# Chunks of the activations without padding, each pair of parts at a place of its own modulo 512 bytes

## The chip, the cores and the metric

The kernel runs on one core of one Trainium2 chip. The metric is the device time of one execution in microseconds. Before the change the median of three runs is 751.33 us (750.96 to 751.88).

## What is computed

The input x has 256 tokens of 1,024 channels. Two different transformer blocks run one after the other, in float32, and a root-mean-square norm stands between them.

The first block: norm, one input projection, then two mixers side by side (block attention with 8 heads of 64 and rotary positions; gated linear attention with 4 heads, a per-token decay and an output gate), a projection w_out back to 1,024 channels and a residual sum. Then norm, an up projection to 2 x 2,816 channels, a causal convolution over 3 tokens, silu(gate) x value, a down projection to 1,024 and a residual sum.

The second block: norm, one input projection that feeds four mixers (short convolution, spatial gating, stick-breaking attention, forgetting attention, each 256 wide) and four gates of 1,024; each mixer's result is projected to 1,024, multiplied with its sigmoid gate and summed; a projection w_out_2 and a residual sum; then a SwiGLU of the same width as the first FFN and a residual sum.

```
h = causal_dwconv(hn @ w_ffn_up, conv_w, conv_b)
x = x + (silu(h_gate) * h_val) @ w_ffn_down
...
merged = sum(gates * branches, axis=2);  h = h + merged @ w_out
h = h + (silu(g) * u) @ w_out_ffn,  g, u = split(norm(h) @ w_ffn_in)
```

## The kernel before

Activations lie with channels on the 128 partitions and tokens along the free axis: 1,024 channels are KD = 8 chunks of 256 tokens, 2,816 channels KF = 22 chunks. A chunk is 256 float32, so 1,024 bytes per partition.

Precision is kept by splitting each operand into a high and a low part: the high part is the value rounded to TensorE's faster float32 form (F32R), the low part the rest. A product is three matmuls (`mm3`, lines 184 to 187): high x high, low x high and high x low. In most stages the weight tile of 128x128 is the stationary operand and a chunk of 128x256 the moving one (`fm`, `fm_pair`); in the four value projections (`tm`) it is the other way round.

The weights, 117 pieces of 1 MB, stream through `raws` (3 buffers) on SP's DMA queue. `Stream.split_to` (lines 145 to 160) makes from each half piece a high part with ScalarE (line 154) and a low part with VectorE (line 155), in `parts`, 5 buffers of 128x1024 each; a half holds 8 weight tiles of 512 bytes per partition. `Stream.tiles` (line 162) hands the tiles out in the order in which the layout on the host has put them, so the order of the matmuls is the order of the program.

The activations' parts live in four tiles of the pool `bigs`, made by `new_x` (xh, xl) and `new_y` (yh, yl), lines 297 to 301. Each such tile has 8 chunks with 8 float32 of padding behind each, so chunk k begins 1,056 k bytes into the tile. They are made anew several times, in the order of the program: xh, xl for the first projections, for the held columns of FFN one, for the mixers' results of the second block (the branches) and for the rest of FFN two; yh, yl for the mixers' results of the first block (w_out), for the rest of FFN one, for the projections of the second block and for the held columns of FFN two. `Boundary` (lines 377 to 424) makes the parts behind each residual sum: first unnormed ones, with which the first HELD = 6 column pairs of the FFN are computed and scaled afterwards, then the normed ones for the other 16. The hidden values of an FFN stand in hh, hl (line 762), 22 chunks with 4 float32 of padding behind each, 1,040 bytes apart. The input of w_out_2, mh and ml (lines 1075 and 1076), has no padding.

Results land in PSUM; VectorE, ScalarE and GpSimd scale, convolve, gate and split them while the next matmuls run. The work of the mixers is written as generators that `pump` advances by a step after every four chunks. lv (line 81) holds the masks that the gated linear attention's six levels read (line 548); its load is one of four in `late_loads` (line 91) on SP's queue.

Of the kernel before, what the change touches and what calls it, by code (L numbers as in the profile page):

```python
# [10 lines left out]
F32R = mybir.dt.float32r  # L11
BF = mybir.dt.bfloat16
I32 = mybir.dt.int32
# [5 lines left out]
D, T, FF = 1024, 256, 2816  # L19
KD, KF = D // 128, FF // 128  # L20
# [7 lines left out]
LEVELS = (1, 2, 4, 8, 16, 32)  # L28
# [24 lines left out]
def block_kernel(ctx: ExitStack, tc: tile.TileContext, xT, wst, sm_d, cs_d, lv_d, gup_d, out, dbg=None):  # L53
    nc = tc.nc
# [3 lines left out]
    def pool(name, bufs, **kw):  # L58
        return tc.tile_pool(name=name, bufs=bufs, reuse_waits="tile", **kw)

    const = ctx.enter_context(tc.tile_pool(name="const", bufs=1))
# [6 lines left out]
    def mm_tile():  # L68
        return mmp.tile([128, 512], F32, name="mm", tag="mm")

    def at_tile():
        return atp.tile([128, 512], F32, name="at", tag="at")
# [5 lines left out]
    X = resid.tile([128, KD, T], F32, name="X")  # L78
    sm = const.tile([128, SM_W], F32, name="sm")
    cs = const.tile([128, CS_W], F32, name="cs")  # L80
    lv = const.tile([128, len(LEVELS), 64], I32, name="lv")
    gup = const.tile([17, 256], F32, name="gup")
    nc.scalar.dma_start(out=sm[:, :SM_FIRST], in_=sm_d[:, :SM_FIRST])

# [6 lines left out]
    def late_loads():  # L91
        nc.sync.dma_start(out=cs, in_=cs_d)
        nc.sync.dma_start(out=sm[:, SM_FIRST:], in_=sm_d[:, SM_FIRST:])
        nc.sync.dma_start(out=lv, in_=lv_d)
        nc.sync.dma_start(out=gup, in_=gup_d)

    def par(name):
# [74 lines left out]
    st = Stream()  # L172
    st.load_to(3)
    late_loads()
    identb = const.tile([128, 128], BF, name="identb")
    V.tensor_copy(identb, ident)
# [12 lines left out]
    def fm(ps, xh, xl, ks, start=True, stop=True, steps=0, **kw):  # L189
        ks = list(ks)  # L190
        for n, k in enumerate(ks):
            wh, wl = st.tiles()
            mm3(ps, wh, wl, xh[:, k, :], xl[:, k, :], start and n == 0, stop and n == len(ks) - 1, **kw)
            if n % 4 == 3:
                pump(steps)

    def fm_pair(ps, xh, xl, between=None):

        for n, (a, k) in enumerate([(a, k) for a in range(2) for k in range(KD - 1)] + [(0, KD - 1), (1, KD - 1)]):
            wh, wl = st.tiles()  # L200
            mm3(ps[:, a * T:(a + 1) * T], wh, wl, xh[:, k, :], xl[:, k, :], n == 0, k == KD - 1,
                skip_group_check=True)
            if between and n == KD:
                between()
# [11 lines left out]
    def split_from(h, l, src):  # L216
        S.copy(h, src)
        V.tensor_tensor(l, src, f32(h), op=ALU.subtract)
# [75 lines left out]

    bigs = ctx.enter_context(tc.tile_pool(name="bigs", bufs=1))

    def new_x():
        return tuple(bigs.tile([128, KD, T + 8], F32R, name=n, tag=n)[:, :, :T] for n in ("xh", "xl"))

    def new_y():  # L300
        return tuple(bigs.tile([128, KD, T + 8], F32R, name=n, tag=n)[:, :, :T] for n in ("yh", "yl"))

    nwk = ctx.enter_context(tc.tile_pool(name="nwk", bufs=1))

# [72 lines left out]
    class Boundary:  # L377


        def __init__(self, g, sums=None, first=None, then=None):  # L380
            self.g, self.then = g, then or new_x
            self.h, self.l = (first or new_y)()
            self.ss = SumSq(nwk, "a")
            self.s2, self.g2 = (SumSq(nwk, "b"), sums) if sums is not None else (None, None)
# [18 lines left out]
        def finish(self):  # L403
            if self.s2 is None:
                v, t = (nwk.tile([128, T], F32, name="sq", tag="sq", bufs=3) for _ in range(2))
                self.rb = nwk.tile([128, T], F32, name="rb", tag="rb", bufs=2)
                V.tensor_scalar(v, self.p1, 1.0 / D, EPS, op0=ALU.mult, op1=ALU.add)
                newton(v, self.rb, t, True)
                return
            else:  # L410
                tc.keep_in_program_order(S.preload_act_table_set("natural_log_exp_and_others"))

                v = nwk.tile([128, 4], F32, name="v4")
                V.tensor_scalar(v[:, 0:2], self.p1, 1.0 / D, EPS, op0=ALU.mult, op1=ALU.add)
                V.tensor_scalar(v[:, 2:4], v[:, 0:2], EPS, None, op0=ALU.mult)
                V.scalar_tensor_tensor(v[:, 2:4], self.p2, 1.0 / D, v[:, 2:4], op0=ALU.mult, op1=ALU.add)
                r = inv_sqrt(v, 4, nwk)
                self.r1, r = r[:, 0:2], r[:, 2:4]
            self.r = r
            self.rb = spread(r, nwk)  # L420
# [6 lines left out]


    with pool("first", 1) as wk:
        ss = SumSq(nwk, "a")  # L430
        xh, xl = new_x()
        for k in range(KD):
            scaled(k, par("g_attn"), xh, xl)
# [16 lines left out]
        V.scalar_tensor_tensor(gq, pss[0].rearrange("p (a t) -> p a t", a=2), 0.125, rbb, op0=ALU.mult, op1=ALU.mult)  # L450
        V.tensor_tensor(gk, pss[1].rearrange("p (a t) -> p a t", a=2), rbb, op=ALU.mult)
        yh, yl = new_y()
        cosr = wk.tile([128, T], F32, name="cosr")
        sinr = wk.tile([128, T], F32, name="sinr")
# [281 lines left out]
        if "ya" in dbg:  # L736
            drain(t_gla)
            for k in range(KD):
                t = wk.tile([128, T], F32, name="dbgt")
# [5 lines left out]
        for half in range(2):  # L745
            for d in range(KD):
                a = accs[d // 2]
                fm(a[:, (d % 2) * T:(d % 2 + 1) * T], yh, yl, range(4 * half, 4 * half + 4),
                   start=(half == 0 and d % 2 == 0), stop=(half == 1), steps=2, skip_group_check=True)
                if half and d % 2:  # L750
                    if d == 1:
                        nb_ = Boundary(par("g_ffn"), first=new_x, then=new_y)
                    for e in (d - 1, d):
                        nb_.add(e, a[:, (e % 2) * T:(e % 2 + 1) * T])
            drain(t_gla)
# [3 lines left out]
    def gated_ffn(nb, emit, finish):  # L759

        with pool("ffn", 1) as wk:
            hh, hl = (wk.tile([128, KF, T + 4], F32R, name=n)[:, :, :T] for n in ("hh", "hl"))
            held = []

            def hidden(ps, j):
                split_from(hh[:, j, :], hl[:, j, :], emit(ps, j, wk))

            for j in range(KF):
                ps = mm_tile()
                if j == 0:  # L770
                    fm_pair(ps, nb.h, nb.l, nb.sums)
                    nb.finish()
                    nb.normed()
                else:
                    x = (nb.h, nb.l) if j < HELD else (nb.xh, nb.xl)
                    for half in range(2):
                        fm(ps[:, half * T:(half + 1) * T], *x, range(KD))
                if j < HELD:
                    t = wk.tile([128, 2, T], F32, name="held", tag="held", bufs=3)
                    V.tensor_tensor(t, ps.rearrange("p (a t) -> p a t", a=2),  # L780
                                    nb.rb[:, None, :].to_broadcast([128, 2, T]), op=ALU.mult)
                    hidden(t.rearrange("p a t -> p (a t)"), j)
                else:
                    hidden(ps, j)
            for d in range(KD):
                ps = mm_tile()
                fm(ps[:, :T], hh, hl, range(KF))
                finish(d, ps[:, :T], wk)
# [24 lines left out]
    def first_end(d, ps, wk):  # L813
        if not holder:
            holder.append(Boundary(ggm, par("g_fin")))
        holder[0].add(d, ps)

    gated_ffn(nb_, conv_emit, first_end)
    nb_ = holder[0]

    with pool("second", 1) as wk:
        yh, yl = new_x()
        fr = [wk.tile([128, 2, T], F32, name="fr", tag="t2", bufs=4) for _ in range(2)]
        pss = []
# [11 lines left out]
        xh, xl, rb, r = nb_.h, nb_.l, nb_.rb, nb_.r  # L839
# [22 lines left out]
        pl = at_tile()  # L862
# [31 lines left out]
        for hd in range(2):  # L894
            p, m = 64 - 64 * hd, 96 - 64 * hd
# [214 lines left out]
        if "yb" in dbg:  # L1110
            for k in range(KD):
                t = wk.tile([128, T], F32, name="dbgt")
# [28 lines left out]
    def second_end(d, ps, wk):  # L1141
        V.tensor_tensor(X[:, d, :], X[:, d, :], ps, op=ALU.add)
        nc.sync.dma_start(out=out[:, d, :], in_=X[:, d, :])

    gated_ffn(nb_, swiglu_emit, second_end)
    assert st.used == 16 * N_PIECES, st.used

# [158 lines left out]
```

## Time and profile before

| | |
|---|---|
| median of three runs | 751.33 us |
| profiled execution | 751.71 us |
| its span | 750.0 us |
| TensorE matmul busy | 736.9 us, 6,042 instructions |
| VectorE busy | 535.8 us |
| ScalarE busy | 423.2 us |
| GpSimd busy | 113.9 us |
| DMA | 127.51 MB, 170 GB/s |
| granted TensorE clock | 0.995 of full speed |

PE is TensorE, PEld its weight loads, DVE VectorE, ACT ScalarE, POOL GpSimd, SP the engine that issues the DMAs. Busy time adds the durations of an engine's instructions, overlaps counted once. A matmul's duration covers its whole way through the array and overlaps the next one's, so the distance between two starts is shorter than a duration. An L with a number is a line of the kernel.

### The profile page before, as it was taken

The page shows a single profiled execution, that of the slowest core. Times are in us where ns is not written, and L with a number is a line of the kernel's source. Part 1 is how long each engine was busy: PE and PEld are TensorE (multiplying, and loading weights), DVE is VectorE, ACT ScalarE, POOL GpSimd, SP SyncE. Part 2 cuts the span into 40 slices and gives each one's busy share as a digit, 9 for nine tenths or more (in the row PEclk, how much of TensorE's full clock was granted, in tenths as well). Part 3 has the DMA queues.
Part 4 walks back from the last instruction along what each step waited for, and adds up shares of the span by engine and source line. Part 5 has one row for each costly group of instructions (what it writes and reads, how often), then busy time and mean ns, then how long its engine had stood idle before and what let it go on. Part 6 is the DMA issues. An engine that isn't in the chain of part 4 may idle for free.

```text
span 750.0 us, 14591 instructions
## 1 busy us (share of the span) xinstructions
PE 736.9 (98%) x6042; PEld 718.9 (96%) x6042; DVE 535.8 (71%) x805; ACT 423.2 (56%) x689; POOL 113.9 (15%) x125
## 2 busy tenths in 40 slices
PE   8997999999999999999999999999999999999998
PEld 7996889999999999999998999999999999999998
DVE  6679756899998776556785787766889855555441
ACT  7574666577767655545457476444467644444330
POOL 3067100214222111221000001100223100000000
PEclk9998999999999999999999999999999999999999
DMA  8742332364555554544443444554446555455530
GB/s 304 291 146 86 113 113 83 143 225 149 189 209 185 189 205 169 176 163 169 169 169 113 169 147 141 198 190 170 169 170 225 177 204 183 173 195 197 188 127 22
DMA packets 19813, 127.51 MB, mean 170 GB/s; under 512 B 2322, under 2 KB 3747, under 8 KB 5027
## 3 DMA queue, kind: packets, MB, share of 16 engines
q1 hardware_dynamic: 19602, 126.56, 47.7%
q8 instruction: 47, 0.77, 0.4%
q14 instruction: 20, 0.16, 0.1%
q10 hardware_dynamic: 144, 0.02, 0.0%
HBM read 125.52 MB, written 1.05 MB: 169 GB/s over the span
## 4 chain that ended last, share of the span: by engine, by line
PE 90%; DVE 6%; ACT 1%; DMA 1%; issue 1%; SPq 0%; DVEq 0%; ACTq 0%
PE mm L185 28%; PE mm L186 28%; PE mm L187 28%; DVE lo L155 2%; DMA X<-in_x 1%; PE at L698 1%; PE at L371 1%; DVE Qb L533 1%; DVE AT L548 1%; PE at L363 1%; DVE xl L283 0%; PE at L927 0%; PE at L372 0%; DVE cv L803 0%; PE at L942 0%
## 5 line engine op out<-in xcount | busy, mean ns | idle before, releaser
L155 DVE TENSOR_TENSOR lo<-raw,hi 128x1024 fp32r<-128x1024 f32 (+1 forms) x236 | 296.2, 1259 | 137.0 <-ACT hi L154 136.1
L154 ACT CAST hi<-raw 128x1024 fp32r<-128x1024 f32 (+1 forms) x236 | 244.5, 1041 | 216.7 <-PE mm L186 170.1
L185 PE MATMUL mm<-yh,hi 128*128 128x256 f32 x800 | 225.0, 283 | 0.8 <-DVE cv L803 0.8
L186 PE MATMUL mm<-yl,hi 128*128 128x256 f32 x800 | 224.0, 281 | 0.0
L187 PE MATMUL mm<-yh,lo 128*128 128x256 f32 x800 | 223.9, 281 | 0.0
L185 PE MATMUL mm<-xh,hi 128*128 128x256 f32 x544 | 153.8, 284 | 1.5 <-ACT hi L154 1.3
L187 PE MATMUL mm<-xh,lo 128*128 128x256 f32 x544 | 153.8, 285 | 1.1 <-DVE lo L155 1.0
L186 PE MATMUL mm<-xl,hi 128*128 128x256 f32 x544 | 152.6, 282 | 0.1
L185 PEld LDWEIGHTS mm<-yh,hi 128*128 128x128 f32 x800 | 150.1, 188 | 1.6 <-ACT hi L154 0.9
L186 PEld LDWEIGHTS mm<-yl,hi 128*128 128x128 f32 x800 | 150.8, 189 | 0.7 <-issue 0.6
L187 PEld LDWEIGHTS mm<-yh,lo 128*128 128x128 f32 x800 | 150.7, 188 | 0.1
L185 PEld LDWEIGHTS mm<-xh,hi 128*128 128x128 f32 x544 | 102.5, 189 | 2.9 <-ACT hi L154 2.1
L187 PEld LDWEIGHTS mm<-xh,lo 128*128 128x128 f32 x544 | 102.5, 189 | 2.8 <-DVE lo L155 2.1
L186 PEld LDWEIGHTS mm<-xl,hi 128*128 128x128 f32 x544 | 102.7, 189 | 0.7 <-DVE xl L283 0.5
L186 PE MATMUL mm<-hl,hi 128*128 128x256 f32 x352 | 99.0, 281 | 0.0
L187 PE MATMUL mm<-hh,lo 128*128 128x256 f32 x352 | 98.8, 281 | 0.0
L185 PE MATMUL mm<-hh,hi 128*128 128x256 f32 x352 | 98.5, 281 | 0.0
L186 PEld LDWEIGHTS mm<-hl,hi 128*128 128x128 f32 x352 | 66.4, 189 | 0.0
L187 PEld LDWEIGHTS mm<-hh,lo 128*128 128x128 f32 x352 | 66.3, 188 | 0.0
L185 PEld LDWEIGHTS mm<-hh,hi 128*128 128x128 f32 x352 | 66.1, 188 | 0.0
L277 POOL TENSOR_TENSOR ssa<-ssa,sq 128x256 f32<-128x256 f32 x20 | 18.7, 936 | 120.9 <-ACT sq L276 120.4
L806 POOL TENSOR_TENSOR cv<-cv 128x256 f32<-128x256 f32 x22 | 23.5, 1067 | 81.0 <-DVE cv L803 76.0
(333 smaller groups left out, 961.3 us busy)
## 6 DMA issues: line engine op xcount, KB each, us to landing
raw<-in_w SPq DMA_DIRECT2D x115, 1024.0 KB, 4.8
raw<-in_w SPq DMA_DIRECT2D x3, 512.0 KB, 8.3
out<-X SPq DMA_DIRECT2D x8, 128.0 KB, 1.9
sm<-in_sm SPq DMA_DIRECT2D x1, 814.5 KB, 13.4
X<-in_x SPq DMA_DIRECT2D x3, 256.0 KB, 7.3
cs<-in_cs SPq DMA_DIRECT2D x1, 706.0 KB, 11.3
raw<-in_w SPq DMA_DIRECT2D x2, 256.0 KB, 4.1
X<-in_x SPq DMA_DIRECT2D x2, 128.0 KB, 3.4
```

Source lines behind the costliest of these rows:

```text
L154: a = S.copy(hi[:, c:c + step], raw[:, c:c + step])
L155: b = V.tensor_tensor(lo[:, c:c + step], raw[:, c:c + step], f32(hi[:, c:c + step]), op=ALU.subtract)
L185: PE.matmul(ps, lh, rh, start=start, stop=False, **kw)
L186: PE.matmul(ps, lh, rl, start=False, stop=False, **kw)
L187: PE.matmul(ps, ll, rh, start=False, stop=stop, **kw)
L277: (V if self.n >= 6 else G).tensor_tensor(self.s, self.s, q, op=ALU.add)
L363: PE.transpose(pts[hd][:, j * 128:(j + 1) * 128], Ps[hd][:, j * 128:(j + 1) * 128], ident)
L371: PE.matmul(o, vs_[hd][0], PTs[hd][:, 0:256], start=True, stop=False, skip_group_check=True)
L533: V.tensor_tensor(q.rearrange("p x (n h) -> p x n h", h=h), qv[rows, :, :, 1, :], ev[rows, :, :, 1, :], op=ALU.mult)
L548: V.copy_predicated(o, lv[:, n, None, :].to_broadcast([128, 8, 64]).rearrange("p e (n h) -> p e n h", h=h), pm.rearrange("p (e n h) -> p e ...
L698: PE.matmul(ps[:, c:c + n], qb[:, a, hd, i * 128:(i + 1) * 128], kT[:, a, :n], start=True, stop=False, skip_group_check=True)
L806: G.tensor_tensor(c[0], c[0], c[1], op=ALU.mult)
```

## The change

The padding of the chunks goes. A helper `placed` makes a tile of n x 256 + 128 float32 and returns a view in which chunk k begins `first` + 256 k float32 into the tile; 256 float32 are 1,024 bytes, so all chunks of a tile have the same place modulo 512 bytes. `new_x` and `new_y` take their pair of starts for the high and the low part from a list, one entry for each time that they are called, and the hidden tiles take theirs in the same way. The order of the entries is the order of use given above. The tile lv moves from the pool `const` into the pool of the first stage, and its load is issued behind the three other late loads.

```diff
-    lv = const.tile([128, len(LEVELS), 64], I32, name="lv")
...
-        nc.sync.dma_start(out=lv, in_=lv_d)
...
+    places = {"x": [(64, 64), (0, 64), (56, 56), (96, 96)], "y": [(80, 48), (32, 32), (64, 64), (64, 0)],
+              "h": [(88, 88), (56, 56)]}
+
+    def placed(pl, name, n, first):
+
+        t = pl.tile([128, n * T + 128], F32R, name=name, tag=name)
+        return t[:, first:first + n * T].rearrange("p (k t) -> p k t", t=T)
+
+    def new_pair(c):
+        return tuple(placed(bigs, c + p, KD, o) for p, o in zip("hl", places[c].pop(0)))
+
     def new_x():
-        return tuple(bigs.tile([128, KD, T + 8], F32R, name=n, tag=n)[:, :, :T] for n in ("xh", "xl"))
+        return new_pair("x")
 
     def new_y():
-        return tuple(bigs.tile([128, KD, T + 8], F32R, name=n, tag=n)[:, :, :T] for n in ("yh", "yl"))
+        return new_pair("y")
...
     with pool("first", 1) as wk:
+        lv = wk.tile([128, len(LEVELS), 64], I32, name="lv")
+        nc.sync.dma_start(out=lv, in_=lv_d)
...
-            hh, hl = (wk.tile([128, KF, T + 4], F32R, name=n)[:, :, :T] for n in ("hh", "hl"))
+            hh, hl = (placed(wk, "h" + p, KF, o) for p, o in zip("hl", places["h"].pop(0)))
```

## Rows read from the trace of the kernel before

**Rows 1.** The head of the page and TensorE's busy time.
```profile
span 750.0 us, 14591 instructions
...
PE 736.9 (98%) x6042; PEld 718.9 (96%) x6042; DVE 535.8 (71%) x805; ACT 423.2 (56%) x689; POOL 113.9 (15%) x125
```

**Rows 2.** The chain that ended last, shares of the span by engine.
```profile
PE 90%; DVE 6%; ACT 1%; DMA 1%; issue 1%; SPq 0%; DVEq 0%; ACTq 0%
```

**Rows 3.** Stretch (us): length, busy PE, PEld, DVE, ACT, POOL; clock, DMA share, GB/s.
```profile
121.60:144.20 22.60, 22.60 (x194) 22.60 (x194) 18.18 (x32) 14.83 (x24) 1.23 (x2) 1.00 0.39 135
144.40:179.80 35.40, 35.24 (x290) 34.47 (x289) 34.00 (x49) 27.01 (x43) 13.27 (x14) 1.00 0.48 168
180.00:271.70 91.70, 90.94 (x769) 90.77 (x769) 83.01 (x130) 61.40 (x104) 19.41 (x18) 1.00 0.55 195
271.90:334.30 62.40, 62.40 (x529) 62.40 (x528) 36.85 (x44) 31.85 (x47) 10.67 (x12) 1.00 0.53 186
...
593.00:683.70 90.70, 90.70 (x769) 90.70 (x769) 51.37 (x67) 43.12 (x64) 0.00 (x0) 1.00 0.55 192
```

**Rows 4.** Order of time, FFN two, columns start us, duration us, instruction.
```profile
652.93 0.28 PE L185 MATMUL mm<-xh,hi 128*128 128x256 f32 x1
652.93 0.19 PEld L186 LDWEIGHTS mm<-xl,hi 128*128 128x128 f32 x1
653.05 0.28 PE L186 MATMUL mm<-xl,hi 128*128 128x256 f32 x1
```

**Rows 5.** Order of time, the first matmul of a stage and of the next, twice.
```profile
271.78 0.28 PE L185 MATMUL mm<-hh,hi 128*128 128x256 f32 x1
...
334.39 0.28 PE L185 MATMUL mm<-yh,hi 128*128 128x256 f32 x1
...
592.93 0.28 PE L185 MATMUL mm<-xh,hi 128*128 128x256 f32 x1
...
683.81 0.28 PE L185 MATMUL mm<-hh,hi 128*128 128x256 f32 x1
```

**Rows 6.** Order of time, TensorE, starts of one turn of eight chunks.
```profile
652.57 0.28 PE L185 MATMUL mm<-xh,hi 128*128 128x256 f32 x1
...
654.36 0.28 PE L185 MATMUL mm<-xh,hi 128*128 128x256 f32 x1
...
655.41 0.28 PE L185 MATMUL mm<-xh,hi 128*128 128x256 f32 x1
```

**Rows 7.** Durations (min/median/max ns) by line, FFN two up, FFN one down.
```profile
L185 PE MATMUL mm<-xh,hi x256: 278/282/286, 592.9 to 683.5; 128*128 128x256 f32 x128
...
L186 PE MATMUL mm<-hl,hi x176: 275/281/286, 271.9 to 334.2; 128*128 128x256 f32 x176
```

**Rows 8.** The unpadded stage: durations by line, first starts there and behind.
```profile
L185 PE MATMUL mm<-mh,hi x64: 280/281/281, 535.9 to 558.1; 128*128 128x256 f32 x64
L186 PE MATMUL mm<-ml,hi x64: 281/281/282, 536.0 to 558.2; 128*128 128x256 f32 x64
...
535.86 0.28 PE L185 MATMUL mm<-mh,hi 128*128 128x256 f32 x1
...
558.47 0.28 PE L185 MATMUL mm<-yh,hi 128*128 128x256 f32 x1
```

**Rows 9.** Waits of VectorE and TensorE for one another, 144 to 272 us.
```profile
PE mm L185 <- DVE cv L803: 0.8, 1, 0.8
```

**Rows 10.** Durations of VectorE's writes of chunks, unpadded and padded tiles.
```profile
L218 DVE TENSOR_TENSOR ml<-gate,mh x8: 410/417/958, 475.7 to 541.9; 128x256 fp32r<-128x256 f32 x8
...
L218 DVE TENSOR_TENSOR hl<-cv,hh x16: 418/419/422, 603.8 to 689.0; 128x256 fp32r<-128x256 f32 x16
```

**Rows 11.** The load of lv and its readers.
```profile
L548 DVE COPY_PREDICATED AT<-lv,at x6: 686/718/1321, 58.9 to 83.0; 128x512 f32<-128x512 int32 x6
L94 SPq DMA_DIRECT2D lv<-in_lv x1: 328/328/328, 10.0 to 10.0; - x1
...
DMA to landing us min/median/max: 12.6/12.6/12.6
```

## The prediction

> **What bounds the kernel now.** I read the head of the page first, then the chain of waits, then the engines' busy time by stage. TensorE is busy for 736.9 of 750.0 us [rows 1] and holds 90% of the chain that ended last [rows 2]. By stage the reader is to see that from 121 us on TensorE has no idle time worth naming: in each of the five stretches shown its busy time equals the length to within 0.8 us, at a granted clock of 1.00 (its upper level, 2.4 GHz), while VectorE and the DMA queues have room [rows 3]. A busy TensorE is not one at its peak, so the next view is the order of time: a matmul of 128x256 lasts 0.28 us, but the next starts 0.12 us later, and the weight load for the next one starts with the matmul [rows 4]. The time is therefore (number of matmuls) x (distance between two starts). I call one such distance a slot. The program has 117 pieces x 16 tiles x 3 = 5,616 slots of this kind.
>
> What a slot lasts: in the second block's wide FFN 768 slots take 683.81 - 592.93 = 90.88 us, 118.3 ns each; in the first block's down projection 528 take 334.39 - 271.78 = 62.61 us, 118.6 ns [rows 5]. Within a stage the slots are not equal. Over one turn of eight chunks the starts of the three-matmul group [rows 6] go 652.57 to 654.36 for five chunks (15 slots, 119.3 ns) and 654.36 to 655.41 for the next three (9 slots, 116.7 ns). The durations say the same in whole ns: 278 to 286 where chunks advance by 32 bytes modulo 512, 275 to 286 where they advance by 16 [rows 7]. The one stage whose chunks are unpadded, and so all stand at one place, has 280 to 282 (two of its three lines shown), and its 192 slots take 558.47 - 535.86 = 22.61 us, 117.8 ns each [rows 8]. So the length of a slot goes with the chunk's place, and a constant place makes it constant.
>
> **The change part by part.**
>
> *The chunks' places.* Before, eight chunks run through eight places modulo 512 (22 places in the hidden tiles), so a stage pays a mean of good and bad ones: 118.3 to 118.6 ns. After, each stage pays one value for the pair it uses. By the tile sizes in the code, all weight tiles begin at one place modulo 512; counted from it in bytes, the new pairs (high, low) and their slots are: first projections (256, 256), 576 slots, of which 192 have x as stationary operand; w_out (320, 192), 192; held FFN columns of block one (0, 256), 288; the rest of its up projection (128, 128), 768; its down projection (256, 256), 528; second block's projections (256, 256), 1,296, of which 144 with x stationary; branches (224, 224), 192; held columns of FFN two (256, 0), 288; the rest (384, 384), 768; its down projection (128, 128), 528. The w_out_2 stage stays at (192, 192), 192 slots [rows 8]. The hidden tiles start 416 bytes on, which is where their 256 and 128 come from.
>
> No stage of before stands still at any of the new places, so their price is bounded. By single matmuls: the constant stage joins 281 ns of duration with a slot of 117.8; durations go from 275 to 286 [rows 7, 8], 6 below and 5 above, so a place could stand for slots of about 112 to 123 ns (an estimate, which takes a ns of duration for a ns of slot). By chunks, which average three matmuls: 116.7 to 119.3 ns. The places' own rows don't decide it, since the same matmul at a chunk lies behind another place there than it will after. The nearest row is the constant stage at 117.8, as after the change every slot also follows a slot at its own place; the pairs also leave out the jump between high and low in the equal pairs. Against the padded mean of 118.4 that is -0.6; the quiet chunks give -1.7. I take the middle, 117.2 ns, or -1.2 per slot: ten pairs are free to lie better than the one that happens to be there, and I give half of that.
>
> Slots that count in full: 5,616 - 192 (unchanged) - 576 (first stage) = 4,848, x 1.2 ns = 5.8 us. The first stage is only partly paced by slots (it lasts to 121.6 us [rows 3], and its 576 slots alone would need 68 us); I count it at half, 576 x 1.2 / 2 = 0.3 us. Sum 6.1 us. Bounds: at 116.7 everywhere 4,848 x 1.7 = 8.2 us gained; at 119.3 everywhere 0.9 x 4,848 = 4.4 us lost; by the single matmuls' ends 112 and 123, some 31 us gained and 22 us lost, which would need every stage at one extreme.
>
> *What is late next.* The weight halves come from ScalarE and VectorE in the shadow of TensorE. At 96% VectorE is nearly full in the held columns of FFN one (34.00 of 35.40 us) and at 91% in the rest of that projection (83.01 of 91.70) [rows 3]; TensorE waited there once, 0.8 us, for VectorE [rows 9]. 1.2 ns of 118.4 is 1.0%, which still fits; 4% would not. If it did not fit, 288 + 768 slots would give nothing: 1.3 us of the 6.1.
>
> *Engines that write the chunks.* VectorE's subtraction that writes a low chunk has a median of 417 ns into the unpadded tile and 419 ns into a padded one [rows 10]; no reader of TensorE's waits for those 2 ns. Nothing.
>
> *The level masks.* The load of lv moves from before gup to after it and into the first stage's pool. It was issued at 10.0 us, landed 12.6 us later and was first read at 58.9 us, some 36 us after [rows 11]. One issue later leaves that cover, so it costs nothing; without the cover the level step at 58.9 us would be late by the difference. gup's load only comes one issue sooner. The pools' places move by multiples of 512 bytes, so all other tiles keep their place modulo 512.
>
> **A rule against this change.** The rows show slots that differ by place while only TensorE's own two streams are regular enough to make a pattern that repeats every turn [rows 6, 7]. The Trainium skill, "SBUF — State Buffer", section "Who interferes with whom", gives TensorE two independent read ports, one for the moving operand and one for weight loads, and says that "PE and ACT never wait on anyone"; by it a place could not matter and the change would do nothing. The trace does not agree: 275 to 286 ns at moving places against 280 to 282 at one.
>
> **The rivals.**
>
> *A. The chosen places are worse than the mean (slower).* Padding insures against a bad place; a constant place removes the insurance. The mechanism is one: (256, 256) carries 528 + 1,296 slots and (128, 128) 768 + 528, so these two pairs decide. For it: high and low at one place and a weight load that always meets the stream at the same point can repeat the worst meeting, and 15 of 24 slots in a turn run at 119.3 [rows 6]. Against: the one constant pair is better than the mean [rows 8]. The price with those 3,120 slots at 121 ns (halfway from 119.3 to the single-matmul end) and the rest as forecast: 3,120 x 2.6 - 1,728 x 1.2 = 8.1 - 2.1 = 6 us slower, 757 us; it decides from a mean over 118.4 ns.
>
> *B. Nothing.* Places do not matter as such; the variation only follows from their changing, and any constant place gives the 118 ns of the mean. For it: the constant stage is 0.6 ns off the mean, not more. Against: it is off. 750 to 752 us.
>
> *C. Quiet places in most stages.* With slots at 115 ns in all 4,848 the gain is 3.4 x 4,848 = 16.5 us, less what VectorE holds back in FFN one (1,056 slots at 117 instead of 115, 2.1 us): 14 us, 737 us. For it: durations down to 275 exist [rows 7]. Against: no chunk as a whole is below 116.
>
> *D. VectorE becomes the bound in FFN one.* The forecast less 1.3 us: 746.5 us. For: 96% [rows 3]. Against: one wait of 0.8 us [rows 9].
>
> **How the numbers follow.** The profiled execution took 751.71 us with a span of 750.0; its sum gives 751.71 - 6.1 = 745.6. The median of the runs is 0.38 below that execution, 751.33, so the forecast is 745.2 us. Chances: the forecast (2 to 10 us faster) 0.40; A 0.25; B 0.13; C 0.17; D 0.05. The range reaches into C and A: 734 (C with a little more) to 757 (A). The likeliest case's own range is 741 to 749.5. A measurement of this kernel tells 0.2%, 1.5 us, from no change. Faster: the forecast, C and D, 0.62; same: B, 0.13; slower: A, 0.25.
>
> **What would show it.** In the changed profile each stage's matmul durations must fall together to one or two ns apart, as they do at 536 us now; if they stay spread, the place is not the cause. The distance between stage starts over the slot count gives each pair's price; equal pairs in two stages, (256, 256) three times and (128, 128) twice, must give equal slots there. The forecast is wrong if these two pairs come out over 118.4 ns, or if waits of TensorE for VectorE appear between 144 and 272 us. A first read of lv that waits for its DMA would show the last step wrong.

## The result and the profile after

The changed kernel takes 755.87 us in the median of four runs (755.77 to 756.06), against 751.61 us for the kernel before in runs beside it: ratio 1.0057, 95% interval 1.0039 to 1.0074. It is slower by 0.6%; 745.2 us was forecast, and the time lies inside the range but on rival A's side. The profiled execution's span grew from 750.0 to 754.0 us.

The head of the page, against [rows 1]: the same number of instructions, 2.0 us more of TensorE's busy time, and the other engines as before.

```profile
span 754.0 us, 14591 instructions
...
PE 738.9 (98%) x6042; PEld 721.2 (96%) x6042; DVE 536.1 (71%) x805; ACT 423.0 (56%) x689; POOL 113.9 (15%) x125
```

The order of time after gives the starts of the stages (start us, duration us, instruction; the lines of the three matmuls are now 183 to 185). They answer to [rows 5, 8].

```profile
272.37 0.28 PE L183 MATMUL mm<-hh,hi 128*128 128x256 f32 x1
...
335.71 0.28 PE L183 MATMUL mm<-yh,hi 128*128 128x256 f32 x1
...
539.08 0.29 PE L183 MATMUL mm<-mh,hi 128*128 128x256 f32 x1
...
561.70 0.28 PE L183 MATMUL mm<-yh,hi 128*128 128x256 f32 x1
...
596.68 0.28 PE L183 MATMUL mm<-xh,hi 128*128 128x256 f32 x1
...
687.82 0.28 PE L183 MATMUL mm<-hh,hi 128*128 128x256 f32 x1
```

Down one, at (256, 256), now takes 335.71 - 272.37 = 63.34 us for 528 slots, 120.0 ns each, where it took 118.6. The second block's projections and branches go from 201.47 to 539.08 - 335.71 = 203.37 us. The rest of FFN two, at (384, 384), takes 91.14 us, 118.7 ns, where it took 118.3. The w_out_2 stage, which the change left alone, has 22.62 us for 192 slots, 117.8 ns, as before. From the same starts in both traces, stage by stage, the change is: first projections +0.33 us, w_out -0.02, held FFN one +0.39, rest of it -0.09, down one +0.74, second projections with branches +1.90, w_out_2 +0.01, held FFN two +0.52, rest +0.26, down two +0.05 (to its last matmul's start). The sum is 4.1 us, the span's growth; 3.5 of it lie in the stages after the first that have a pair made of 256 and 0.

The durations, answering to [rows 7, 8]: down one, the rest of FFN two and w_out_2 (min/median/max ns), and last the weight loads of down one.

```profile
L184 PE MATMUL mm<-hl,hi x173: 281/283/283, 272.8 to 334.8; 128*128 128x256 f32 x173
...
L184 PE MATMUL mm<-xl,hi x254: 279/281/285, 596.8 to 686.9; 128*128 128x256 f32 x127
...
L184 PE MATMUL mm<-ml,hi x60: 281/281/281, 539.9 to 560.8; 128*128 128x256 f32 x60
...
L184 PEld LDWEIGHTS mm<-hl,hi x173: 187/192/192, 273.1 to 335.0; 128*128 128x128 f32 x173
```

Before, the weight loads of down one had 187/188/193:

```profile
L186 PEld LDWEIGHTS mm<-hl,hi x174: 187/188/193, 272.1 to 333.7; 128*128 128x128 f32 x174
```

So at (256, 256) the median weight load takes 192 ns, near the longest of before. At (384, 384) the place is constant and the durations still spread from 279 to 285. The order of time in the rest of FFN one, at (128, 128), shows why:

```profile
220.16 0.28 PE L184 MATMUL mm<-yl,hi 128*128 128x256 f32 x1
220.28 0.28 PE L185 MATMUL mm<-yh,lo 128*128 128x256 f32 x1
220.40 0.28 PE L183 MATMUL mm<-yh,hi 128*128 128x256 f32 x1
220.52 0.28 PE L184 MATMUL mm<-yl,hi 128*128 128x256 f32 x1
220.64 0.28 PE L185 MATMUL mm<-yh,lo 128*128 128x256 f32 x1
220.75 0.28 PE L183 MATMUL mm<-yh,hi 128*128 128x256 f32 x1
```

To within 1 ns the distances there are 118, 121, 120, 119, 115 and again (the rows give 10 ns; the trace's starts are in whole ns): a turn of five slots in a program that goes by threes. A slot does not depend on its place alone; it also depends on the slot before it, and a constant place gives a rhythm, which need not be one constant length.

### The profile page after: what moved, and what is told of

Read it like the earlier page. It is cut to its first block, busy times and chain, and to the rows that moved or that the text cites. A ratio compares the mean times of both kernels' runs of the same rounds, so it can differ in the third digit from the quotient of the medians.

```text
span 754.0 us, 14591 instructions
## 1 busy us (share of the span) xinstructions
PE 738.9 (98%) x6042; PEld 721.2 (96%) x6042; DVE 536.1 (71%) x805; ACT 423.0 (56%) x689; POOL 113.9 (15%) x125
## 4 chain that ended last, share of the span: by engine, by line
PE 85%; DVE 10%; issue 2%; ACT 1%; DMA 1%; SPq 0%; DVEq 0%; ACTq 0%
PE mm L184 26%; PE mm L183 26%; PE mm L185 26%; DVE lo L153 4%; DVE cv L815 1%; PE at L381 1%; DVE cv L814 1%; DMA X<-in_x 1%; DVE Qb L545 1%; DVE AT L560 1%; PE at L373 1%; PE at L710 1%; DVE xl L281 1%; ACT hi L152 0%; DVE held L792 0%
```

## The experiments

The theories: P, a slot's length belongs to the pair of places counted from the weights' place, and the pairs at 256 and 0 are bad; Q, standing still is what costs, wherever; R, the move of lv or of the pools did it; S, the activations' own place decides, whatever the weights'. In most runs only the list `places` of the changed kernel is edited, and after the first fence only the new lines are shown; the pairs are given here in bytes from the weights' place. The uninterrupted slots of a stage are the distances under 130 ns with no other work of TensorE between the two starts.

**1. Ten pairs at once, e1_map_equal and e2_map_more** (one profiled execution each). The edit of the first and of the second:

```diff
-    places = {"x": [(64, 64), (0, 64), (56, 56), (96, 96)], "y": [(80, 48), (32, 32), (64, 64), (64, 0)],
-              "h": [(88, 88), (56, 56)]}
+    places = {"x": [(36, 36), (4, 4), (44, 44), (24, 24)], "y": [(28, 28), (8, 8), (12, 12), (20, 20)],
+              "h": [(40, 40), (64, 64)]}
```
```diff
+    places = {"x": [(48, 48), (52, 52), (48, 48), (48, 80)], "y": [(16, 48), (80, 48), (48, 48), (60, 60)],
+              "h": [(8, 8), (104, 104)]}
```

> Every stage gets an equal pair (high and low at one place) that no run has stood at: in bytes from the weights' place 144 first projections, 112 w_out, 16 held FFN one, 32 rest of FFN one, 64 down one, 48 second projections, 176 branches, 80 held FFN two, 96 rest of FFN two, 160 down two. Theory P (a slot's length belongs to the pair of places, counted from the weights): the ten stages show different lengths, some under 117, some near 120; within a stage the slots repeat in a short cycle. Rival Q (standing still is what costs, wherever): all stages between 118.5 and 120 ns as after the change, total 754 to 757 us.

> Pairs (high, low) by stage: first (192,192), w_out (64,192), held FFN one (208,208), rest of FFN one (320,192), down one (448,448), second projections (192,192), branches (192,192), held FFN two (240,240), rest of FFN two (192,320), down two (320,320). Theory P: every (192,192) stage has 117.8 ns as w_out_2 has; (320,192) has 117.8 for 768 slots too, as it has for 192 after the change; if the pattern repeats every 256 bytes, (448,448) in down one gives 117.8 as well, if every 512 it need not. Rival Q: 118.5 to 120 in all of them; 117.8 then belongs to the w_out_2 stage and not to the place.

748.43 and 739.89 us, with the kernel before at 751.71. Down one at (64, 64), in the first (the first matmul of it and of the next stage, then durations), against the rest of FFN two at (96, 96):

```profile
270.62 0.28 PE L183 MATMUL mm<-hh,hi 128*128 128x256 f32 x1
...
330.46 0.28 PE L183 MATMUL mm<-yh,hi 128*128 128x256 f32 x1
...
L184 PE MATMUL mm<-hl,hi x175: 276/276/276, 270.7 to 329.9; 128*128 128x256 f32 x175
...
L184 PEld LDWEIGHTS mm<-hl,hi x174: 187/188/188, 271.0 to 329.8; 128*128 128x128 f32 x174
...
L184 PE MATMUL mm<-xl,hi x254: 279/282/286, 588.8 to 679.9; 128*128 128x256 f32 x127
```

By the stage starts the first has 59.84 us for 528 slots, 113.3 ns, and no weight load above 188 ns; the second 120.0 ns. Of the others w_out at 112 has 114.7, the rest of FFN one at 32 118.3 (waits included; 116.7 uninterrupted) and down two at 160 118.7. In the second kernel down one at (448, 448) also has 113.4, the rest of FFN one and two at (320, 192) and (192, 320) 119.0 (waits included; 117.8 uninterrupted) and 117.8, down two at (320, 320) 117.8. P stands and Q falls: the places differ by 7 ns. What neither had foreseen: w_out_2, untouched at (192, 192), ran at 113.5 and 113.3 ns here where it had 117.8 in both kernels compared. The second projections at (192, 192), in the second kernel, had 114.4 on the mean of their uninterrupted slots with a chunk moving, so P's one price of 117.8 for that place fails.

**2. All pairs at (192, 192), e3_all_192** (six executions).

```diff
+    places = {"x": [(48, 48)] * 4, "y": [(48, 48)] * 4, "h": [(72, 72)] * 2}
```

> All pairs at (192,192), the place of the one stage that the change left alone. Theory P: all slots near 117.8 ns against 118.4 before: 4,848 x 0.6 = 2.9 us faster than before, about 748.5 us, ratio 0.996. Rival Q: as after the change, 755 us, ratio 1.005. Rival R (the move of lv or the shift of the pools made it slower, not the places): slower than before by about 4 us whatever the places, 755 us.

Six executions of this one program took 741.79, 741.78, 742.34, 737.27, 736.74 and 730.68 us; the kernel before stayed between 750.9 and 752.1. The granted clock was 0.995 to 1.000 in all six. None is near the 755 us of Q and R, and all lie below the 748.5 us that P forecast from one price. The profiled one (741.79 us) shows both lengths at one place: the first matmul of down one and of the next stage, matmuls and weight loads, then the same of w_out_2.

```profile
269.90 0.28 PE L183 MATMUL mm<-hh,hi 128*128 128x256 f32 x1
...
332.09 0.28 PE L183 MATMUL mm<-yh,hi 128*128 128x256 f32 x1
...
L184 PE MATMUL mm<-hl,hi x176: 281/281/282, 270.0 to 331.9; 128*128 128x256 f32 x176
...
L184 PEld LDWEIGHTS mm<-hl,hi x176: 187/192/193, 269.9 to 331.7; 128*128 128x128 f32 x176
...
527.81 0.28 PE L183 MATMUL mm<-mh,hi 128*128 128x256 f32 x1
...
549.57 0.28 PE L183 MATMUL mm<-yh,hi 128*128 128x256 f32 x1
...
L184 PE MATMUL mm<-ml,hi x63: 276/276/277, 527.9 to 549.0; 128*128 128x256 f32 x63
...
L184 PEld LDWEIGHTS mm<-ml,hi x64: 187/188/188, 527.8 to 549.2; 128*128 128x128 f32 x64
```

117.8 and 113.3 ns at the same pair of places in one execution. In the slower rhythm one weight load of the three in a turn takes 192 ns, that of the line shown; the other two lines have a median of 188, as in the faster one. In this trace the rhythm lasts over hundreds of slots and across stages, and changes only near an interruption (a wait, or the mixers' small matmuls) or, once, where the value projections end. So (192, 192) has two rhythms, and the 117.8 that the prediction took as the place's price was one of them. Only this execution was traced; that the faster three had more of the short rhythm is inferred, and the size allows it: the fastest is close to what 112 takes with 113.3 ns nearly everywhere (experiment 6).

**3. lv alone, e4_lv_only** (ten executions): the kernel before, padding kept, with the load of lv and its tile moved as in the change.

```diff
-    lv = const.tile([128, len(LEVELS), 64], I32, name="lv")
...
+        lv = wk.tile([128, len(LEVELS), 64], I32, name="lv")
+        nc.sync.dma_start(out=lv, in_=lv_d)
```

> The kernel before with lv alone moved, padding kept. Theories P and Q: as before, 751.5 us within 0.2%. Rival R: about 755 us.

751.54 us, ratio 1.0001 (0.9992 to 1.001). R falls.

**4. Who is counted from whom: e5_weights_64 and e6_all_moved_64** (four executions each). In the first the weights' tiles move by 64 bytes (with them the raw pieces and some constants) and the activations by 512, in the second weights and activations together by 64 (the two lines of `shift` only).

```diff
+    back = resid.tile([128, 112], F32, name="back")
+    nc.gpsimd.memset(back, 0.0)
     X = resid.tile([128, KD, T], F32, name="X")
...
+    shift = const.tile([128, 16], F32, name="shift")
+    nc.gpsimd.memset(shift, 0.0)
```

> The changed kernel with the weights' tiles alone moved by 64 bytes (64 bytes of padding before them, 448 behind, so that all activations keep their place modulo 512). Counted from the weights every place falls by 64: the pairs (256,256) become (192,192), (128,128) become (64,64), the w_out_2 stage (192,192) becomes (128,128). Theory P, relative to the weights: no stage keeps the flat 120 ns of (256,256); those stages have one of the two lengths that (192,192) showed, 113.3 or 117.7; w_out_2 goes to 118.7 as (128,128) has; total 725 to 750 us. Rival S (the activations' own place decides, whatever the weights'): all stages as after the change, 756 us.

> The changed kernel with the weights and all activations moved together by 64 bytes. Theory P: the pairs counted from the weights are unchanged, so every stage is as after the change, 120 ns at (256,256) and 118.7 at (128,128), 755.9 us within 0.3%. Rival S: other lengths in all stages, a total that differs.

743.0 us, ratio 0.9876 (0.9858 to 0.9895), and 755.56 us, ratio 1.0053 (1.0038 to 1.0068). With the weights moved, down one and w_out_2, whose activations lie where they lay in the changed kernel:

```profile
L188 PE MATMUL mm<-hl,hi x173: 281/281/281, 271.0 to 331.8; 128*128 128x256 f32 x173
...
L188 PE MATMUL mm<-ml,hi x61: 279/281/285, 529.4 to 550.7; 128*128 128x256 f32 x61
```

Down one left the flat 283 for the slower rhythm of (192, 192), 117.8 ns by its starts, and w_out_2 took on the spread of (128, 128), 118.6 ns by its starts. With everything moved, down one has the changed kernel's row again:

```profile
L186 PE MATMUL mm<-hl,hi x175: 281/283/283, 272.1 to 334.7; 128*128 128x256 f32 x175
```

S falls: the distance between the moving operand's place and the weights' decides.

**5. Only the pairs at 256 and 0 moved, to (64, 64): e8_no_256** (six executions), and finer places: **e7_map_fine** (one profiled execution).

```diff
+    places = {"x": [(16, 16), (16, 16), (56, 56), (96, 96)], "y": [(80, 48), (32, 32), (16, 16), (16, 16)],
+              "h": [(40, 40), (56, 56)]}
```
```diff
+    places = {"x": [(112, 112), (22, 22), (112, 112), (14, 14)], "y": [(16, 16), (28, 28), (28, 28), (26, 26)],
+              "h": [(42, 42), (54, 54)]}
```

> The changed kernel with only the pairs at 256 or 0 (first projections, held FFN one and two, down one, second projections) put to (64,64); the pairs (320,192), (128,128), (224,224), (384,384) as changed. Theory P: those 2,400 slots and the first 576 go from 120 to 113.3 or 117.7, so 5 to 18 us faster than after the change, 738 to 751 us; the stages at (128,128) and (384,384) stay at 118.7. Rival Q (standing still costs, not the place): 756 us.

> Equal pairs at new places: 448 first projections and branches, 64 w_out, 88 held FFN one, 112 rest of FFN one and second projections, 72 down one, 104 held FFN two, 56 rest of FFN two, 120 down two. Theory P with two rhythms: 448 and 64 show 113.3 or 117.7 by stretches and nothing else; one of 56, 72, 104, 112, 120 might hold 114 throughout (112 did so for 192 slots of w_out). Rival Q (no place is steady and fast, 113 is chance): all new places between 117 and 120.

e8_no_256: 748.99 us, ratio 0.9966 (0.9953 to 0.9978), so 6.9 us below the changed kernel, from +0.6% to -0.3%. Its down one has 117.8 ns, its rest of FFN two at (384, 384) 118.7 as after the change. The loss sat in the pairs at 256 and 0; by the stage starts 0.8 us of the 6.9 come from w_out_2, which fell into its faster rhythm. Down one, in the slower rhythm here, has no weight load above 188 ns in any of its three lines, so loads of 192 ns are not what makes that rhythm:

```profile
L184 PEld LDWEIGHTS mm<-hl,hi x176: 187/188/188, 271.0 to 332.8; 128*128 128x128 f32 x176
```

e7_map_fine: 745.45 us. 8 bytes decide: the rest of FFN one at 112 and down one at 72, with the first matmul of down one and of the next stage.

```profile
L184 PE MATMUL mm<-yl,hi x256: 275/275/282, 180.2 to 268.5; 128*128 128x256 f32 x128
...
L184 PE MATMUL mm<-hl,hi x176: 278/285/287, 268.9 to 332.8; 128*128 128x256 f32 x176
...
268.77 0.28 PE L183 MATMUL mm<-hh,hi 128*128 128x256 f32 x1
...
333.02 0.28 PE L183 MATMUL mm<-yh,hi 128*128 128x256 f32 x1
```

72 gives 121.7 ns a slot (64.25 us for 528), 8 bytes from the 64 that gave 113.3 in e1_map_equal and 117.8 in e8_no_256; 56 gives 118.4, 120 gives 120.2, 88 and 104 give 120.0 uninterrupted. None of these five places off a multiple of 16 bytes is below 118.4, but 96 and 256, which are multiples, have 120.0 too; whether the 16 bytes matter by themselves no run separates. At 112 the second block's projections with a chunk moving stayed near 113 ns through all their interruptions too (114.0 on the mean of the uninterrupted slots).

**6. All pairs at 112: e9_all_112** (four executions), **at 368: e10_all_368** (four), **at 112 with the first projections at 448: e11_112_first_448** (five).

```diff
+    places = {"x": [(28, 28)] * 4, "y": [(28, 28)] * 4, "h": [(52, 52)] * 2}
```
```diff
+    places = {"x": [(92, 92)] * 4, "y": [(92, 92)] * 4, "h": [(116, 116)] * 2}
```
```diff
+    places = {"x": [(112, 112)] + [(28, 28)] * 3, "y": [(28, 28)] * 4, "h": [(52, 52)] * 2}
```

> All pairs at (112,112), the place that held 113.4 ns in rest of FFN one, in the second projections and in w_out. Theory P: every stage with a chunk as moving operand at 113.5 ns, the value projections (x stationary) at 119.9 as second projections' showed; against before 4,704 x 4.9 = 23 us, some 4 of the first stage, less 336 x 1.5 = 0.5 us: 725 to 730 us, and one length in all executions within 0.3%. Rival two rhythms everywhere: stages at 113 and 118 in a mix, executions several us apart, 730 to 742 us as at (192,192).

> All pairs at (368,368), which is 112 + 256. If the pattern repeats every 256 bytes, as 0 and 256, and 128 and 384, suggest: as (112,112), 725 to 730 us. If it repeats every 512 only: other lengths, no forecast, 730 to 757 us.

> As all at (112,112), with the first projections at (448,448), whose value projections ran at 116 ns instead of 119.9 but whose chunk matmuls may fall into the slower rhythm of 117.7 after an interruption. Theory P: 192 x 3.7 = 0.7 us from the value projections, at most 384 x 2 = 0.8 us back: within 0.2% of all at (112,112). Rival (the first stage is paced by VectorE, not by slots): the same, to 0.1%.

730.94 us (ratio 0.9725, 0.9711 to 0.9738), 731.73 (0.9733, 0.972 to 0.9746) and 730.21 (0.9721, 0.9708 to 0.9734): 2.7 to 2.8% faster than before, and each kernel's executions within 0.3% of one another. Rest of FFN two, all at 112: matmuls and weight loads, and its starts, 87.04 us for 768 slots, 113.3 ns.

```profile
L184 PE MATMUL mm<-xl,hi x256: 275/275/275, 579.1 to 665.8; 128*128 128x256 f32 x128
...
L184 PEld LDWEIGHTS mm<-xl,hi x256: 187/188/188, 579.0 to 665.7; 128*128 128x128 f32 x128
...
579.01 0.28 PE L183 MATMUL mm<-xh,hi 128*128 128x256 f32 x1
...
666.05 0.28 PE L183 MATMUL mm<-hh,hi 128*128 128x256 f32 x1
```

At 368 the same stage has the same row, 275/275/275, so the pattern repeats every 256 bytes. The totals lie just above the expected 725 to 730 us; the third run does not separate its two theories, which forecast the same total. The next bound shows in the first of the three: stretches of held FFN one and of its rest (columns as in [rows 3]), and TensorE's waits there (us in total, times, longest).

```profile
143.80:178.40 34.60, 34.20 (x292) 33.44 (x291) 33.40 (x46) 26.58 (x43) 12.78 (x14) 1.00 0.45 171
178.50:268.40 89.90, 87.69 (x769) 87.12 (x768) 82.19 (x132) 61.62 (x106) 24.47 (x18) 1.00 0.57 200
```
```profile
PE mm L183 <- DVE cv L815: 1.9, 1, 1.9
PE mm L185 <- DVE lo L153: 0.6, 2, 0.3
```

In the held columns VectorE fills 33.40 of 34.60 us, and they still gained (35.66 us by the starts before, 34.61 here). The rest of FFN one takes 90.09 us by its starts where 768 slots of 113.3 would take 87.0, 2.5 of the 3.1 in these waits. That is rival D in part, at a gain large enough to meet it.

At 368 one more loss stands behind this wait. In the traced execution there, TensorE was busy for 0.31 of 2.20 us around its wait of 1.9 us (first row, columns as above), and 1.3 us after it worked again the granted clock fell to 0.51, the lower of its two levels (second row). Slots took 213 ns there, some 1.6 us lost by the starts. The traced execution at 112 stayed at 1.00 behind the same wait, so the wait alone does not settle it.

```profile
200.20:202.40 2.20, 0.31 (x3) 0.13 (x2) 2.20 (x6) 1.78 (x4) 0.00 (x0) 1.00 0.77 324
203.70:207.00 3.30, 3.30 (x18) 3.30 (x17) 3.30 (x6) 2.33 (x5) 0.73 (x1) 0.51 0.56 151
```

## Why the prediction was wrong

*What bounds the kernel, and that a slot's length goes with its place: right, though the place alone does not fix it.* The change moved the slots and nothing else; lv cost nothing (experiment 3), the writes of the chunks and the other engines are as before.

*The failed step is the price of the new places*, "I take the middle, 117.2 ns, or -1.2 per slot". Over the stages after the first the span grew by 3.8 us, +0.8 ns for each of the 4,848 slots instead of -1.2. Two things were wrong in it. The nearest row, w_out_2 at 117.8, was one of two rhythms of a place that none of the new pairs has, and said nothing of the others: equal pairs measured here run from 113.3 to 121.7 ns. And the allowance for places that "are free to lie better" had no row behind it; the ends of 112 and 123 that stood beside it were the honest price, and by them the sign was open. By the uninterrupted slots no new pair but w_out's (117.8 against 117.9) came out below the padded chunks that it replaced.

*"A constant place makes it constant": wrong.* It held at (256, 256), and fails at (128, 128) and (384, 384), a rhythm of five lengths, and at (192, 192), two rhythms. The check given, durations within one or two ns in every stage, fails in the stages at 128 and 384 for this reason and not because the place does not matter; the other check, equal pairs giving equal slots, held (120.0 ns in down one and 119.8 on the mean of the uninterrupted slots of the second projections; 118.7 in both stages at (128, 128), uninterrupted). Both pairs are over 118.4, the sign that the prediction gave for its being wrong.

*Rival A was the right one, for half of its place.* (256, 256) did settle at 120.0 ns, near A's 121; (128, 128) settled at 118.7 (without the waits of FFN one), 0.1 to 0.4 ns above the stages before. What A missed is that (0, 256) and (256, 0) are the same case: with a pattern of 256 bytes, 0 and 256 are one place. A's 757 us was 1.1 us too high, and that it came so near is partly luck: by the stage starts A's two pairs cost 2.6 us where it charged 8.1, and the other changed stages behind the first cost 1.1 us where it gave back 2.1.

*B fell* (places differ by 8 ns). *C's* quiet places exist, and 112, at 113.3 ns, is below C's 115, but no stage of the change stood there. *D* did not come up, as there was no gain to hold back: TensorE waited for VectorE once between 144 and 272 us, 0.4 us.

*The rule.* The Trainium skill ("SBUF — State Buffer", "Who interferes with whom") says that TensorE's two read ports are independent and that TensorE never waits on anyone. Experiment 4 goes against what the prediction took from it, that a place could not matter: moving the weights' tiles by 64 bytes against the activations changed the matmuls' slots (down one from 120.0 to 117.8 ns), and moving all together left them. That the two reads meet in the memory is what these rows suggest; no run looks inside it, and why 112 has one rhythm where 192 has two stays open.

## What to carry to other kernels

When one engine runs back to back, divide a stage's time by its count before calling it full: a slot of 118 ns at 98% busy hid 4% here. Padding that spreads chunks over places gave 118.3 to 118.6 ns here, between the 113.3 and 121.7 of constant places; a constant place can be better or worse, so measure several places in one kernel, a stage each, before choosing, and repeat the run, since one place can have two rhythms. A place that was read in one execution of one stage is not a price.

## What the runs showed that was not expected

- Slots of a weight load and a float32 matmul of 128x256 at the upper clock run between 113.3 and 121.7 ns, by the distance of the moving operand's place from the weights', with a period of 256 bytes (0 and 256, 112 and 368, 128 and 384, 192 and 448 agree); 8 bytes can cost 4 or 8 ns (64, in its slower or faster rhythm, against 72).
- One program with one set of inputs took 730.7 to 742.3 us; its one trace shows two rhythms at (192, 192), 113.3 and 117.8 ns.
- With the operands' roles exchanged (x stationary), 112 is the bad place: 119.6 to 119.7 ns an uninterrupted slot in the value projections, against 115.5 and 116.1 at 448, and moving the first projections to 448 made no difference beyond the measurement (730.94 against 730.21 us).
